# A matmul kernel for a hybrid decoder layer: weights asked for buffer by buffer, attention heads cut into more steps, gates' outcome in place

## The chip, the cores and the metric

The kernel runs on one core of a Trainium2 chip. The metric is the device time of one execution in microseconds (us); the kernel before takes 1519.82 us, the median of 3 runs (1517.38 to 1522.48). TensorE is PE in the profile, VectorE DVE, ScalarE ACT, GpSimd POOL, and SyncE, which issues most of the DMAs, SP.

## The reference, cut to what matters

```python
h = einsum('bsd,dc->bsc', x, w_in) + b_in             # 1024 tokens, 2048 -> 4352
q, k, v, g_attn, u_pool, g_pool = split(h)            # 16 heads of 64, 2 kv heads
a = banded_sink_attention(q, k, v, sinks, bias) * silu(g_attn)   # window 128
b = multiscale_pool(u_pool, w_pool, pool_scale) * silu(g_pool)
mix = einsum('bsc,cd->bsd', concat([a, b]), w_out)    # 2048 -> 2048
ple = sigmoid(x @ w_gate_ple) * (p @ w_ple)
return layer_norm(2**0.25 * x + mix + ple, ln_gain, ln_bias)
```

Everything is float32. In the attention, per head and block of 128 queries, the scores against the previous and the present 128 keys get a relative-position bias; the softmax takes a sink into its sum.

## The kernel before, in words

A float32 product is made of three matmuls in a reduced format: each operand is split into a high part (a cast on ACT) and a low part (a subtraction on DVE), and high x high, high x low and low x high are added in PSUM (`mm3`). Two blocks of 128 output rows and one half of the contraction make a *job*. Seven products (p1 to p7) of block sums take the place of eight, and a product is twelve matmuls with 512 columns. Their left operand is a *unit*: a 128x512 piece of the weights, or of sums of such pieces, split into `wh` (ACT, L213) and `wl` (DVE, L120) four products before its use (`take`, `units_to`). The raw weights come as two 512 KB buffers for a job out of a pool of five (`raw`). A job's results are gathered from the PSUM banks `qa`, `qb` and `sc` into an SBUF buffer `part` of 128x1024, by an ACT copy (L337) the first time and a DVE addition after that.

The stages, in order of time: two groups and then 25 jobs for the first projection (queries, keys and values first, then gates); 20 jobs for its other half of the contraction, where attention gates, pooling and the embedding are applied; the output projection in two halves; a last part with 256 columns; the layer norm. The program is written as one Python loop. A *tick* is the end of one product: `after(n, fn)` runs `fn` n ticks later, `later(n, fn)` does so too and puts its instructions behind the latest marked ones of PE, ACT and DVE. A scheduler then orders the instructions of each engine by when their inputs should be there, with the order of the program as priority; an engine runs its instructions strictly in that order.

Beside the first stage's last 24 jobs run the 16 attention heads, one every 9 ticks (`heads`). `begin` fetches a head's queries from DRAM (`s<-q`) and splits them at once, two casts on ACT (L479, L481) and two subtractions on DVE; `score` multiplies with the keys; `softmax` takes the exponential (ACT L516), adds the two halves (POOL), and scales by one over the sum (ACT L526); `trans` transposes. Small buffers `s` come from a pool of 16. In the same stretch `centre_weights` goes twice over half of w_out in 256 KB pieces through the only buffer `cw`: fetch, subtract the mean (DVE, L120), store to `wc`.

Where the second stage ends, the attention gates' last four blocks are done: `gate_ahead` fetches the attention results (`s<-pre`, two halves per block), `gate_attn` takes Silu of the part (ACT L586), multiplies the fetched halves in place (DVE, `s<-s,part`), and stores each half of 256 KB to `cc` with a DMA on POOL's queue. The pool of small buffers is cut to four there, and `gate_ahead` is called when a job's last product is done. At the first of the plain jobs `norm_scale` and then `norm_out` of the first layer norm are put between products.

Of the kernel before, what the change touches and what calls it, by code (L numbers as in the profile page):

```python
# [31 lines left out]
P = 128  # L32
T = 512
# [17 lines left out]
F1, F2 = 768, 256  # L51

# [10 lines left out]
class Layer:  # L63
    def __init__(self, ctx, tc, x, p, win, wgate, wout, wple, wpool, cst, rel, out):
        self.tc, self.nc = tc, tc.nc
        self.x, self.p, self.wple, self.wpool, self.rel, self.out = x, p, wple, wpool, rel, out
        self.win, self.wgate, self.wout = win, wgate, wout
        self.ctx = ctx
        self.dram = self.pool("dram", 1, space=DRAM)
        self.ps = self.pool("ps", 1, space=PSUM)  # L70
        self.fix = self.pool("fix", 1)
        self.sm = self.pool("sm", 3)
        self.wp = self.pool("w", 4)
        self.rp = self.pool("r", 5)
# [11 lines left out]
        self.n_raw = self.n_split = self.n_used = 0  # L86
# [101 lines left out]
    def load_raw(self, job):  # L188
        if id(job) not in self.raw:
            self.raw[id(job)] = [self.tile(self.rp, [P, 2 * H], "raw") for _ in range(2)]  # L190
            for i in range(2):
                self.load(self.raw[id(job)][i], job.w[job.b[i], job.half])

    def make_unit(self, i):
        job, o = self.seq[i]
        L, nc = self, self.nc
        self.load_raw(job)
        r0, r1 = self.raw[id(job)]
# [4 lines left out]
        if o in ("p5", "p6") and id(job) not in self.s1:  # L203

            s1 = self.s1[id(job)] = self.tile(self.sp, [P, H], "s1")
# [4 lines left out]
        src = {"p1": a11, "p2": a12, "p5": self.s1.get(id(job)), "p6": a11, "p7": a21, "p3": a12, "p4": a22,  # L210
# [5 lines left out]
        if o in ("p4", "a22"):  # L216
            self.raw[id(job)] = None
# [137 lines left out]
    def run_group(self, g, steps=(), then=None):  # L355

        jobs, order = self.groups[g]
        ahead = [j for js, _ in self.groups[g + 1 : g + 2] for j in js]
        st = {}
        for i, job in enumerate(jobs):  # L360
            self.load_raw(job)
# [48 lines left out]
    def run_plain(self, g):  # L410

        (job,), order = self.groups[g]
        self.load_raw(job)
        for js, _ in self.groups[g + 1 : g + 2]:
            self.load_raw(js[0])
        for i in range(2):
            ps = self.bank(BANKS[0][i], 2)[:, :F2]
            for u in range(2):
# [6 lines left out]
                self.mark("PE", mm)  # L425
                if u:
# [40 lines left out]
    def heads(self, h, j):  # L467
# [3 lines left out]
        qs, sc, pt, pv, pre, bias = [], {}, {}, {}, [], []  # L471

        def begin():
            rq = self.fetch(self.qd[j][:, h * T : h * T + T])
            bias.append(self.slot()[:, :T].rearrange("p (e k) -> p e k", e=2))
            self.load(bias[0], self.rel[j])
            qs.extend([self.slot(F32R), self.slot(F32R)])
            a, b = slice(0, 64), slice(64, 128)
            nc.scalar.copy(out=qs[0][a, :T], in_=rq[a, :T])  # L479
            self.lo(qs[0][b, :T], rq[a, :T], qs[0][a, :T])  # L480
            nc.scalar.copy(out=qs[1][b, :T], in_=rq[b, :T])  # L481
            self.lo(qs[1][a, :T], rq[b, :T], qs[1][b, :T])
# [29 lines left out]
        def softmax(bq):  # L512
# [57 lines left out]
        begin()  # L570
        for bq in range(4):
            t = 4 * (bq // 2)
            self.after(3 + 2 * bq, lambda bq=bq: score(bq))
            if bq % 2:
                self.after(7 + t, lambda bq=bq: shift(bq - 1))
                self.after(13 + t, lambda bq=bq: trans(bq - 1))
            self.after(8 + t, lambda bq=bq: softmax(bq))
            self.after(18 + t + bq % 2, lambda bq=bq: value(bq))
# [200 lines left out]
    def norm_scale(self, L):  # L779
# [16 lines left out]
        self.norm_spread(L, L["a"], self.ones, dg)  # L796
# [13 lines left out]
    def run(self):  # L810
# [63 lines left out]
        for j in s3:  # L874
            j.wait = 3 if j in s3[-2:] else 4
            j.ahead = self.embed_ahead if j.w is wgate else (lambda b: self.gate_ahead(b - GA0)) if j.b[0] < U0 else None
# [43 lines left out]
        for job in s1[:3]:  # L920
            self.raw[id(job)] = [self.tile(self.rp if job is not s1[2] or i else r1, [P, 2 * H], "raw") for i in range(2)]

        def piece(job, t, f):
            self.load(self.raw[id(job)][t][:, f], job.w[job.b[t], job.half][:, f])
# [53 lines left out]
        for i in range(16):  # L978
            self.after(t + 9 * i, lambda i=i: self.heads(i % 2, i // 2))
# [12 lines left out]
        for i in range(n3):  # L992
# [7 lines left out]
            if i == n3 - 1:  # L1000
# [190 lines left out]
```

## Time and profile before

| what | us |
|---|---|
| median of 3 runs | 1519.82 |
| profiled execution | 1519.77 |
| its span, first to last instruction | 1517.8 |
| TensorE busy | 1455.6 (96%) |
| VectorE busy | 1122.1 (74%) |
| ScalarE busy | 784.4 (52%) |
| GpSimd busy | 281.8 (19%) |
| mean granted TensorE clock | 0.985 |

The profiled execution is 0.05 us from the median, and 1.97 us of it lie outside the span. TensorE is the busiest engine by far, so what it waits for, and the stretches in which it runs at the lower clock, are what a change can take away without taking away matmuls. In a timeline the bracket at the end of a row gives the time that the engine sat idle before it, and who let it go.

### The profile page before, as it was taken

To read this page: it belongs to the slowest core of one execution; us is meant where nothing else is said; L and a number is where in the kernel's file an instruction comes from. 1 tells how busy PE (TensorE), PEld (TensorE's weight loads), DVE (VectorE), ACT (ScalarE), POOL (GpSimd) and SP (SyncE) were. 2 spreads that over 40 slices of the span, in tenths; PEclk is the share of its full clock that TensorE was granted. 3 is DMA by queue.
4 is the path that set the end of the run, shared out by engine and by line. 5 is a ranking of instruction groups with operands and counts; after the bars stand their busy time and mean duration, and the time that the engine had idled before them with its cause. 6 is when DMAs were issued, how large, how long until landed. Compare 5 with 4: busy or idle time off the path is not lost. (4 is left out here: it accounts for less than half of the span.)

```text
span 1517.8 us, 20491 instructions
## 1 busy us (share of the span) xinstructions
PE 1455.6 (96%) x6972; PEld 1227.7 (81%) x6972; DVE 1122.1 (74%) x2030; ACT 784.4 (52%) x1550; POOL 281.8 (19%) x396
## 2 busy tenths in 40 slices
PE   8999899999998999999999998999997999999986
PEld 6788688888877888878887786888886888899985
DVE  7787478788787788788666785565658766987786
ACT  5463556565655656566544453333336433554485
POOL 0001123323322333231111111000012111111240
PEclk9999999999999999999999999999999999999998
DMA  6563875445554456447767657675759578585564
GB/s 259 204 218 100 216 186 194 166 140 166 170 172 161 165 187 200 167 158 259 170 179 194 177 138 242 178 189 164 202 179 291 136 185 234 139 249 126 152 227 148
DMA packets 101848, 280.37 MB, mean 185 GB/s; under 512 B 11760, under 2 KB 17008, under 8 KB 101744
## 3 DMA queue, kind: packets, MB, share of 16 engines
q1 hardware_dynamic: 76400, 199.89, 39.4%
q0 software_dynamic: 19840, 67.64, 19.4%
q10 hardware_dynamic: 5504, 11.54, 2.2%
q8 instruction: 54, 0.88, 0.2%
q14 instruction: 50, 0.41, 0.1%
HBM read 193.04 MB, written 85.98 MB: 184 GB/s over the span
## 5 line engine op out<-in xcount | busy, mean ns | idle before, releaser
L213 ACT CAST wh<-raw 128x512 fp32r<-128x512 f32 x428 | 263.9, 619 | 404.1 <-PE qa L178 136.1
L120 DVE TENSOR_TENSOR wl<-raw,wh 128x512 fp32r<-128x512 f32 x428 | 296.4, 697 | 147.7 <-ACT wh L213 140.8
L337 ACT COPY part<-qa 128x512 f32<-128x512 f32 (+1 forms) x180 | 103.8, 577 | 42.9 <-PE qa L179 42.3
L542 POOL TENSOR_SCALAR_AFFINE_SELECT s<-s 128x512 fp32r<-128x512 f32 x128 | 102.1, 809 | 115.1 <-ACT s L535 84.2
L177 PE MATMUL qa<-t2h,wh 128*128 128x512 f32 (+1 forms) x260 | 102.5, 395 | 15.7 <-ACT wh L213 9.8
L120 DVE TENSOR_TENSOR part<-part,qb 128x512 f32<-128x512 f32 (+1 forms) x120 | 80.9, 674 | 47.7 <-PE qb L179 47.6
L177 PE MATMUL qa<-b11h,wh 128*128 128x512 f32 (+2 forms) x292 | 111.1, 381 | 2.1 <-ACT b11h L239 1.5
L179 PE MATMUL qa<-b11h,wl 128*128 128x512 f32 (+2 forms) x292 | 110.0, 377 | 1.1 <-DVE wl L120 1.1
L178 PE MATMUL qa<-b11l,wh 128*128 128x512 f32 (+2 forms) x292 | 110.0, 377 | 0.2 <-DVE b11l L120 0.2
L177 PE MATMUL qb<-b21h,wh 128*128 128x512 f32 (+2 forms) x292 | 109.1, 374 | 0.0
L179 PE MATMUL qb<-b21h,wl 128*128 128x512 f32 (+2 forms) x292 | 108.7, 372 | 0.1
L178 PE MATMUL qb<-b21l,wh 128*128 128x512 f32 (+2 forms) x292 | 108.6, 372 | 0.0
L179 PE MATMUL qa<-t2h,wl 128*128 128x512 f32 (+1 forms) x260 | 100.8, 388 | 4.0 <-DVE wl L120 4.0
L177 PE MATMUL qb<-t1h,wh 128*128 128x512 f32 (+1 forms) x260 | 101.8, 392 | 2.5 <-DVE part L120 1.1
L177 PE MATMUL qa<-t3h,wh 128*128 128x512 f32 (+1 forms) x260 | 101.0, 389 | 2.6 <-ACT part L337 2.5
L177 PE MATMUL qa<-t4h,wh 128*128 128x512 f32 (+1 forms) x260 | 100.5, 386 | 1.9 <-DVE part L120 1.9
L179 PE MATMUL qb<-t1h,wl 128*128 128x512 f32 (+1 forms) x260 | 100.5, 386 | 1.5 <-DVE wl L120 1.5
L177 PE MATMUL qb<-b22h,wh 128*128 128x512 f32 (+1 forms) x260 | 100.7, 387 | 0.0
L178 PE MATMUL qb<-t1l,wh 128*128 128x512 f32 (+1 forms) x260 | 100.4, 386 | 0.0
L178 PE MATMUL qa<-t2l,wh 128*128 128x512 f32 (+1 forms) x260 | 100.4, 387 | 0.0
L179 PE MATMUL qb<-b22h,wl 128*128 128x512 f32 (+1 forms) x260 | 99.8, 384 | 0.0
L178 PE MATMUL qa<-t4l,wh 128*128 128x512 f32 (+1 forms) x260 | 99.7, 384 | 0.0
(285 smaller groups left out, 3575.1 us busy)
## 6 DMA issues: line engine op xcount, KB each, us to landing
raw<-in_win SPq DMA_DIRECT2D x65, 512.0 KB, 4.1
h<-part SPq DMA_DIRECT2D x34, 512.0 KB, 3.0
part<-h POOLq DMA_DIRECT2D x34, 512.0 KB, 6.4
cw<-in_wout SPq DMA_DIRECT2D x64, 256.0 KB, 3.0
raw<-in_wgate SPq DMA_DIRECT2D x32, 512.0 KB, 4.1
raw<-wc SPq DMA_DIRECT2D x32, 512.0 KB, 4.4
s<-in_x SPq DMA_DIRECT2D x44, 256.0 KB, 5.0
wc<-cw SPq DMA_DIRECT2D x32, 256.0 KB, 2.2
```

Source lines behind the costliest of these rows:

```text
L120: return (eng or self.nc.vector).tensor_tensor(out=out, in0=a, in1=b, op=op)
L177: mm(ps, wh, xh, start=start, stop=False, skip_group_check=True)
L178: mm(ps, wh, xl, start=False, stop=False, skip_group_check=True)
L179: return mm(ps, wl, xh, start=False, stop=stop, skip_group_check=True)
L213: self.unit_latest = [nc.scalar.copy(out=hi, in_=src).ins, L.lo(lo, src, hi).ins]
L337: self.mark("ACT", self.nc.scalar.copy(out=dst, in_=ps))
L542: nc.gpsimd.affine_select(out=o4, in_=a4, pattern=[[0, 4], [sign, P]], compare_op=ALU.is_ge, fill=0.0, base=0 if side else -1, channel_mul ...
```

## The change

Raw weights: `load_raw`, which asks for both buffers of a job at a set product of the group before, becomes `feed_raw`, which after every product asks for the next buffer if the unit that last reads the buffer five before has been made (`freed`, `ring`).

Heads: `begin` comes a tick earlier and only fetches; the casts and subtractions of the queries become `split`, three ticks later and behind the marked instructions. The scaling by one over the sum becomes `share`, two ticks after `softmax` and behind the marked instructions. The rest of a head stays at the same tick as before.

Gates: the product goes into the part (`c[:, h]`), and one 512 KB DMA stores both halves. For the last two jobs `gate_ahead` is called 4 to 7 ticks after the last group begins, not when a job ends; the small pool there has 6 buffers of 512 columns in place of 4 of 528, and `two` 8 in place of 9.

Layer norm: the spreading matmuls of the first `norm_scale` come two ticks later, and `norm_out` runs from tick 7 on, two a tick, in place of 3 in two ticks from tick 5.

```diff
-    def load_raw(self, job):
-        if id(job) not in self.raw:
-            self.raw[id(job)] = [self.tile(self.rp, [P, 2 * H], "raw") for _ in range(2)]
-            for i in range(2):
-                self.load(self.raw[id(job)][i], job.w[job.b[i], job.half])
+    def feed_raw(self, until=None):
+        while self.to_feed:
+            job, i = self.to_feed[0]
+            if self.ring[-RAWS] not in self.freed and (until is None or (until, 1) in self.ring):
+                return
+            self.to_feed.pop(0)
+            t = self.tile(self.rp, [P, 2 * H], "raw")
+            self.raw.setdefault(job, []).append(t)
+            self.load(t, job.w[job.b[i], job.half])
+            self.ring.append((job, i))
...
-        if o in ("p4", "a22"):
-            self.raw[id(job)] = None
+        if o in ("p3", "a12", "p4", "a22"):
+            self.freed.add((job, int(o in ("p4", "a22"))))
...
                 self.product(job, o, st[job])
-                if i == (0 if g else 2) and job is jobs[-1]:
-                    for j in ahead:
-                        self.load_raw(j)
+                self.feed_raw()
...
         def begin():
-            rq = self.fetch(self.qd[j][:, h * T : h * T + T])
+            rq.append(self.fetch(self.qd[j][:, h * T : h * T + T]))
             bias.append(self.slot()[:, :T].rearrange("p (e k) -> p e k", e=2))
             self.load(bias[0], self.rel[j])
+
+        def split():
+            q = rq[0]
             qs.extend([self.slot(F32R), self.slot(F32R)])
-            nc.scalar.copy(out=qs[0][a, :T], in_=rq[a, :T])
+            nc.scalar.copy(out=qs[0][a, :T], in_=q[a, :T])
...
             if z == 0:
                 self.tt(cur, old, cur, ALU.add, nc.gpsimd)
+
+        def share(bq):
+            cur = sc[bq][:, :, P:]
             for e in range(2):
...
         begin()
+        self.later(3, split)
...
-            self.after(3 + 2 * bq, lambda bq=bq: score(bq))
+            self.after(4 + 2 * bq, lambda bq=bq: score(bq))
...
-            self.after(8 + t, lambda bq=bq: softmax(bq))
-            self.after(18 + t + bq % 2, lambda bq=bq: value(bq))
+            self.after(9 + t, lambda bq=bq: softmax(bq))
+            self.later(11 + t, lambda bq=bq: share(bq))
+            self.after(19 + t + bq % 2, lambda bq=bq: value(bq))
...
         for h, pre in enumerate(self.got.pop(("ga", j))):
-            f = slice(h * T, h * T + T)
-            self.tt(pre, pre, c[:, h], ALU.mult)
-            self.aside(self.cc[j // 2][:, j % 2, f], pre)
+            self.tt(c[:, h], pre, c[:, h], ALU.mult)
+        self.aside(self.cc[j // 2][:, j % 2], c.rearrange("p h t -> p (h t)"))
...
+        spread = lambda: self.norm_spread(L, L["a"], self.ones, dg)
+        if wait:
+            self.later(wait, spread)
...
-            self.after(t + 9 * i, lambda i=i: self.heads(i % 2, i // 2))
+            self.after(t - 1 + 9 * i, lambda i=i: self.heads(i % 2, i // 2))
...
-                self.slots = self.work_pool("slots1", 4, work)
-                self.twos = self.work_pool("twos1", 9, work)
+                self.slot_n = T
+                self.slots = self.work_pool("slots1", 6, work)
+                self.twos = self.work_pool("twos1", 8, work)
                 pooled()
+                for n, b in enumerate(b for j in s3[-2:] for b in j.b):
+                    self.after(4 + n, lambda b=b: self.gate_ahead(b - GA0))
...
-        self.later(4, lambda: self.norm_scale(one))
+        self.later(4, lambda: self.norm_scale(one, 2))
         for j in range(NB):
-            self.later(5 + (2 * j) // 3, lambda j=j: self.norm_out(one, j))
+            self.later(7 + j // 2, lambda j=j: self.norm_out(one, j))
```

How the change moves instructions is seen at three places. The names carry a buffer's number, the brackets name what an instruction waits for (DMAHW and DMASW are DMAs of SP and of POOL, PE, DVE, Activation and Pool the engines), and "..." stands for rows left out.

First place: ACT in the second group of the second stage, where the first head begins. Before, the queries' casts (`s_1620`, `s_1621`) stand among the units and ahead of the keys' build (`kh`) and of the copies `part<-qa`:

```order
L213 CAST wh_1510<-raw_1426 128x512 [waits DVE_49,PE_49]
L479 CAST s_1620<-s_1616 64x512 [waits DMAHW7_49]
L213 CAST wh_1536<-raw_1426 128x512 [waits DVE_49,PE_49,Activation_49]
L481 CAST s_1621<-s_1616 64x512
L213 CAST wh_1571<-s_359_1531 128x512 [waits PE_49,Activation_49]
L337 COPY part_1407<-qa_1412 128x512 [waits PE_49]
L123 ACTIVATE s_1506<-s_1506,cst 64x512 [waits DMASW6_49]
L123 ACTIVATE s_1507<-s_1507,cst 64x512 [waits DMASW7_49,DMASW5_49,DMASW3_49]
L442 CAST kh_362_1556<-s_1506 64x512 [waits Activation_49]
L442 CAST kh_362_1556<-s_1506 64x512
...
L337 COPY part_1569<-qa_1575 128x512 [waits DMASW2_49,DMASW0_49,PE_49]
```

In the changed kernel:

```order
L222 CAST wh_1516<-raw_1312 128x512 [waits DVE_49,PE_49]
L222 CAST wh_1542<-raw_1312 128x512 [waits DVE_49,PE_49,Activation_49]
L222 CAST wh_1577<-s_362_1537 128x512 [waits PE_49,Activation_49]
L346 COPY part_1413<-qa_1418 128x512 [waits PE_49]
L125 ACTIVATE s_1512<-s_1512,cst 64x512 [waits DMASW6_49]
L125 ACTIVATE s_1513<-s_1513,cst 64x512 [waits DMASW7_49,DMASW5_49,DMASW3_49]
...
L445 CAST kh_367_1569<-s_1513 64x512
L346 COPY part_1575<-qa_1581 128x512 [waits DMASW2_49,DMASW0_49,PE_49]
...
L346 COPY part_1576<-qb_1660 128x512 [waits DMAHW5_49,PE_49]
L485 CAST s_1676<-s_1596 64x512 [waits DMAHW7_49]
L487 CAST s_1677<-s_1596 64x512
```

The two casts (now L485 and L487) have gone behind the keys' build and behind the copies of both banks, some twenty rows later.

Second place: SP in the middle of the heads, in the second pass of `centre_weights` over w_out. Before:

```order
L134 DMA cw_4527<-in_wout 128x512 [waits DMAHW1_49,DMAHW0_49]
L134 DMA raw_4789<-in_wgate 128x1024 [waits DVE_49]
L134 DMA wc_207<-cw_4527 128x512 [waits DMAHW3_49,DMAHW1_49,DVE_49]
L134 DMA raw_5034<-in_wgate 128x1024 [waits DMAHW4_49,DVE_49]
L134 DMA cw_4599<-in_wout 128x512 [waits DMAHW3_49]
L134 DMA pre_157<-s_4496 128x512 [waits DMAHW6_49,DVE_49]
L134 DMA wc_208<-cw_4599 128x512 [waits DMAHW7_49,DMAHW5_49,DVE_49]
```

In the changed kernel:

```order
L136 DMA g_131<-part_4252 128x1024 [waits Activation_49]
L136 DMA cw_4523<-in_wout 128x512 [waits DMAHW7_49,DMAHW1_49]
L136 DMA wc_207<-cw_4523 128x512 [waits DMAHW2_49,DMAHW1_49,DVE_49]
L136 DMA raw_4591<-in_wgate 128x1024 [waits DMAHW3_49,DVE_49]
L136 DMA cw_4599<-in_wout 128x512 [waits DMAHW2_49]
L136 DMA raw_4639<-in_wgate 128x1024 [waits DVE_49]
```

The store `wc_207<-cw` stood between two raw loads, with the next `cw` fetch behind the second of them; now store, raw load, fetch, raw load follow each other.

Third place: where the second stage ends. ACT before, with the four Silus (L586) of the gates' last parts and the first copies into the next group's parts:

```order
L337 COPY part_10796<-qa_10818 128x512 [waits PE_49]
L586 ACTIVATE part_10484<-part_10484,cst 128x1024 [waits DMASW0_49]
L586 ACTIVATE part_10485<-part_10485,cst 128x1024 [waits DMASW2_49,Activation_49]
L213 CAST wh_10847<-s_2128_10842 128x512 [waits DVE_49]
L337 COPY part_10798<-qa_10851 128x512 [waits DVE_49,PE_49,Activation_49]
L586 ACTIVATE part_10486<-part_10486,cst 128x1024 [waits DMASW1_49]
L586 ACTIVATE part_10487<-part_10487,cst 128x1024 [waits DMASW3_49]
L239 CAST t2h_10928<-two_10506 128x1024 [waits DVE_49]
L239 CAST t2h_10928<-two_10507 128x1024 [waits DVE_49]
```

In the changed kernel:

```order
L346 COPY part_10794<-qa_10816 128x512 [waits DMASW3_49,PE_49]
L597 ACTIVATE part_10484<-part_10484,cst 128x1024 [waits DMASW4_49]
L597 ACTIVATE part_10485<-part_10485,cst 128x1024 [waits DMASW6_49,Activation_49]
L248 CAST t2h_10918<-two_10506 128x1024 [waits DVE_49]
L346 COPY part_10796<-qa_10847 128x512 [waits DMASW0_49,PE_49,Activation_49]
L597 ACTIVATE part_10486<-part_10486,cst 128x1024 [waits DMASW5_49]
L597 ACTIVATE part_10487<-part_10487,cst 128x1024 [waits DMASW7_49]
L222 CAST wh_10882<-s_2135_10877 128x512 [waits DVE_49]
L222 CAST wh_10900<-raw_10375 128x512 [waits PE_49]
L248 CAST t2h_10918<-two_10507 128x1024
L346 COPY part_10795<-qb_10930 128x512 [waits DMASW1_49,PE_49,Activation_49]
```

The copies `part<-qa` and `part<-qb` now wait for DMAs of POOL (the stores of the gates' outcome out of the part that they are to fill), and one of them stands ahead of the last two Silus. SP at the same place, before:

```order
L134 DMA raw_10534<-in_wout 128x1024 [waits DMAHW4_49,DVE_49]
L134 DMA raw_10537<-in_wout 128x1024 [waits DMAHW5_49,DVE_49]
L134 DMA raw_10538<-in_wout 128x1024 [waits DMAHW6_49,DVE_49]
L134 DMA raw_10865<-in_wout 128x1024 [waits DMAHW7_49,DVE_49]
L134 DMA s_10787<-pre_160 128x512 [waits DMAHW0_49,DMASW4_49,DVE_49]
L134 DMA s_10789<-pre_160 128x512 [waits DMAHW1_49,DMASW5_49,DVE_49]
L134 DMA s_10792<-pre_161 128x512 [waits DMAHW2_49,DMASW6_49,DVE_49]
L134 DMA s_10794<-pre_161 128x512 [waits DMAHW3_49,DMASW7_49,DVE_49]
```

In the changed kernel:

```order
L136 DMA s_10634<-pre_160 128x512 [waits DMAHW7_49]
L136 DMA s_10636<-pre_160 128x512 [waits DMAHW0_49]
L136 DMA raw_10680<-in_wout 128x1024 [waits DMAHW6_49,DVE_49]
L136 DMA raw_10716<-in_wout 128x1024 [waits DMAHW7_49,DVE_49]
L136 DMA raw_10718<-in_wout 128x1024 [waits DMAHW0_49,DVE_49]
L136 DMA raw_10737<-in_wout 128x1024 [waits DMAHW1_49,DVE_49]
L136 DMA s_10659<-pre_161 128x512 [waits DMAHW2_49,DVE_49]
L136 DMA s_10661<-pre_161 128x512 [waits DMAHW3_49,DVE_49]
```

The fetches of the attention's results (`s<-pre`) wait for no DMA of POOL any more, and six of the eight are ahead of the four raw loads, where four were.

## Rows read from the trace of the kernel before

**Rows 1.** The page, part 1: busy time, share of the span, instructions.

```profile
PE 1455.6 (96%) x6972; PEld 1227.7 (81%) x6972; DVE 1122.1 (74%) x2030; ACT 784.4 (52%) x1550; POOL 281.8 (19%) x396
```

**Rows 2.** Windows, by stretch: length, then each engine's busy time, granted clock, DMA share.

```profile
170.00:185.00 15.00, 9.52 (x35) 7.35 (x35) 8.13 (x13) 10.01 (x18) 0.89 (x1) 0.77 0.63 135
405.00:435.00 30.00, 27.68 (x138) 22.78 (x137) 23.05 (x56) 20.49 (x51) 9.84 (x14) 1.00 0.54 185
475.00:485.00 10.00, 4.91 (x20) 4.48 (x21) 7.04 (x16) 5.05 (x12) 2.85 (x4) 0.66 0.56 195
630.00:640.00 10.00, 8.41 (x43) 6.85 (x42) 5.22 (x12) 4.07 (x7) 1.96 (x4) 1.00 0.64 221
665.00:685.00 20.00, 17.53 (x84) 14.12 (x83) 13.25 (x31) 12.68 (x35) 8.90 (x11) 1.00 0.49 154
1165.00:1185.00 20.00, 12.13 (x42) 9.11 (x41) 18.49 (x25) 8.46 (x12) 2.70 (x5) 0.74 0.40 135
```

**Rows 3.** Waits of ACT and DVE: total us, times, longest.

```profile
ACT s L479 <- DMA s<-q: 39.8, 13, 8.7
DVE cw L120 <- DMA cw<-in_wout: 12.1, 7, 4.7
```

**Rows 4.** Timeline of ACT, 162 to 179 us: start, length, instruction, idle before.

```profile
172.08 0.62 ACT L479 CAST s<-s 64x512 fp32r<-64x512 f32 x1 [8.69 <-DMA s<-q]
174.89 1.33 ACT L123 ACTIVATE s<-s,cst 64x512 f32<-64x512 f32 x2
176.12 2.53 ACT L442 CAST kh<-s 64x512 fp32r<-64x512 f32 x4
178.68 0.59 ACT L337 COPY part<-qa 128x512 f32<-128x512 f32 x1
```

**Rows 5.** Timeline of PE at the same place.

```profile
173.44 0.39 PE L179 MATMUL qb<-b21h,wl 128*128 128x512 f32 x1
179.32 0.79 PE L177 MATMUL qa<-t2h,wh 128*128 128x512 f32 x1 [5.49 <-ACT part L337]
184.33 0.60 PE L454 MATMUL tr<-ident,s 128*128 128x128 f32 x4
```

**Rows 6.** Timeline of SP at the same place: the store and the fetch.

```profile
159.51 2.10 SPq L134 DMA_DIRECT2D q<-part  x2
167.05 0.32 SPq L134 DMA_DIRECT2D s<-q  x1
```

**Rows 7.** Timeline of PE, 420 to 426 us.

```profile
424.88 0.33 PE L500 MATMUL sc<-kl,s 128*128 128x128 f32 x1 [1.04 <-DVE kl L120]
```

**Rows 8.** Timeline of SP, 463 to 470 us: the centring's store and next fetch.

```profile
463.60 0.33 SPq L134 DMA_DIRECT2D wc<-cw  x1
469.55 0.33 SPq L134 DMA_DIRECT2D cw<-in_wout  x1
```

**Rows 9.** Timeline of DVE, 472 to 478 us.

```profile
472.73 0.69 DVE L120 TENSOR_TENSOR cw<-cw,wmean 128x512 f32<-128x512 f32 x1 [4.67 <-DMA cw<-in_wout]
```

**Rows 10.** Timeline of PE, 474 to 485 us.

```profile
480.09 1.11 PE L454 MATMUL tr<-ident,s 128*128 128x128 f32 x4 [5.16 <-DVE s L120]
```

**Rows 11.** Timeline of SP, POOL, DVE and PE where the stage of gates ends.

```profile
1165.48 3.88 SPq L134 DMA_DIRECT2D s<-pre  x4
...
1162.53 1.23 POOL L139 DMA_DIRECT2D cc<-s  x2 [3.30 <-DVE s L120]
...
1170.57 1.41 DVE L120 TENSOR_TENSOR s<-s,part 128x512 f32<-128x512 f32 x2 [0.58 <-DMA s<-pre]
...
1175.74 0.80 PE L177 MATMUL qa<-t2h,wh 128*128 128x512 f32 x1 [1.15 <-ACT wh L213]
```

**Rows 12.** DMA issues: KB each and median us to landing.

```profile
cc<-s POOLq DMA_DIRECT2D x32, 256.0 KB, 4.1
co<-part POOLq DMA_DIRECT2D x16, 512.0 KB, 5.8
```

**Rows 13.** Timeline of PE at the first layer norm's scale.

```profile
1455.32 1.56 PE L776 MATMUL sc<-q,ones 128*128 128x512 f32 x4 [1.34 <-ACT q L794]
```

More of the change, by code (lines that the diff above doesn't have):

```diff
@@ L51 @@
 F1, F2 = 768, 256
+RAWS = 5
 class Job:
@@ L196, in make_unit @@
         L, nc = self, self.nc
-        self.load_raw(job)
-        r0, r1 = self.raw[id(job)]
+        if len(self.raw.get(job, ())) < 2:
+            self.feed_raw(job)
+        r0, r1 = self.raw[job]
         a11, a12, a21, a22 = r0[:, :H], r0[:, H:], r1[:, :H], r1[:, H:]
@@ L202, in make_unit @@
             behind.enter_context(self.tc.issue_after(ins))
-        if o in ("p5", "p6") and id(job) not in self.s1:
-            s1 = self.s1[id(job)] = self.tile(self.sp, [P, H], "s1")
+        if o in ("p5", "p6") and job not in self.s1:
+            s1 = self.s1[job] = self.tile(self.sp, [P, H], "s1")
             L.tt(s1, a21, a22, ALU.add)
@@ L209, in make_unit @@
             L.tt(a12, a12, a11, ALU.subtract)
-        src = {"p1": a11, "p2": a12, "p5": self.s1.get(id(job)), "p6": a11, "p7": a21, "p3": a12, "p4": a22,
+        src = {"p1": a11, "p2": a12, "p5": self.s1.get(job), "p6": a11, "p7": a21, "p3": a12, "p4": a22,
                "a11": a11, "a12": a12, "a21": a21, "a22": a22}[o]
@@ L357, in run_group @@
         jobs, order = self.groups[g]
-        ahead = [j for js, _ in self.groups[g + 1 : g + 2] for j in js]
         st = {}
         for i, job in enumerate(jobs):
-            self.load_raw(job)
             st[job] = dict(tags=BANKS[i], out=[self.new_part(b) for b in job.b], filled=job.filled)
@@ L425, in run_plain @@
                 self.mark("PE", mm)
+                self.feed_raw()
                 if u:
@@ L470, in heads @@
         mx, neg, sk, den, rec = (st[:, 8 * i : 8 * i + 8] for i in range(5))
-        qs, sc, pt, pv, pre, bias = [], {}, {}, {}, [], []
+        rq, qs, sc, pt, pv, pre, bias = [], [], {}, {}, {}, [], []
         def begin():
-            rq = self.fetch(self.qd[j][:, h * T : h * T + T])
+            rq.append(self.fetch(self.qd[j][:, h * T : h * T + T]))
             bias.append(self.slot()[:, :T].rearrange("p (e k) -> p e k", e=2))
             self.load(bias[0], self.rel[j])
+        def split():
+            q = rq[0]
             qs.extend([self.slot(F32R), self.slot(F32R)])
             a, b = slice(0, 64), slice(64, 128)
-            nc.scalar.copy(out=qs[0][a, :T], in_=rq[a, :T])
-            self.lo(qs[0][b, :T], rq[a, :T], qs[0][a, :T])
-            nc.scalar.copy(out=qs[1][b, :T], in_=rq[b, :T])
-            self.lo(qs[1][a, :T], rq[b, :T], qs[1][b, :T])
+            nc.scalar.copy(out=qs[0][a, :T], in_=q[a, :T])
+            self.lo(qs[0][b, :T], q[a, :T], qs[0][a, :T])
+            nc.scalar.copy(out=qs[1][b, :T], in_=q[b, :T])
+            self.lo(qs[1][a, :T], q[b, :T], qs[1][b, :T])
         def k0(bq):
@@ L777, in norm_spread, with norm_scale @@
             self.nc.scalar.activation(out[:, i:e], ps, AF.Copy, scale=scale)
-    def norm_scale(self, L):
+    def norm_scale(self, L, wait=0):
         nc, n = self.nc, L["n"] // P
@@ L875, in run @@
             j.wait = 3 if j in s3[-2:] else 4
-            j.ahead = self.embed_ahead if j.w is wgate else (lambda b: self.gate_ahead(b - GA0)) if j.b[0] < U0 else None
+            j.ahead = self.embed_ahead if j.w is wgate else (lambda b: self.gate_ahead(b - GA0)) if j.b[0] < U0 and j.wait == 4 else None
         mixed = [(wout, *p) for p in pairs(0, 8)]
@@ L920, in run @@
         for job in s1[:3]:
-            self.raw[id(job)] = [self.tile(self.rp if job is not s1[2] or i else r1, [P, 2 * H], "raw") for i in range(2)]
+            self.raw[job] = [self.tile(self.rp if job is not s1[2] or i else r1, [P, 2 * H], "raw") for i in range(2)]
+        every = [(j, i) for js, _ in self.groups for j in js for i in range(2)]
+        self.ring = [k for k in every[:6] if k != (s1[2], 0)]
+        self.to_feed = every[6:]
         def piece(job, t, f):
-            self.load(self.raw[id(job)][t][:, f], job.w[job.b[t], job.half][:, f])
+            self.load(self.raw[job][t][:, f], job.w[job.b[t], job.half][:, f])
         lo, up, all_ = slice(0, H), slice(H, 2 * H), slice(0, 2 * H)
```

15 lines of the change are left out of this document (7 added, 8 removed).

## The prediction

> **What bounds the kernel now.** I read the busy times first: TensorE works 96% of the span [rows 1], so only the other 4%, some 60 us, and the stretches at the lower clock can be won; the change takes no matmul away. Then I laid windows over the span and kept those in which PE falls short of its window and in which the changed code runs [rows 2]. The reader is to see two kinds: windows at clock 1.00 that miss 1 to 3 us, and three (170–185, 475–485, 1165–1185) that miss 5 to 8 us and have a clock of 0.66 to 0.77 besides. The waits then say who stands in the way: ACT's cast of a head's queries waits 39.8 us for the fetch, DVE's centring 12.1 us for its piece of w_out [rows 3]. Both engines run in order, so what counts is what is queued behind. The timelines at the three places give that.
>
> **The change, part by part.** The sum is made against the profiled execution, 1519.77 us, which is 0.05 us from the median of the runs.
>
> *Queries' split, first head.* Two queries' stores start at 159.51 and the fetch that reads one back can only go at 167.05 [rows 6]. ACT stands 8.69 us for it, until 172.08 [rows 4]. Behind the cast are queued three units, two bias additions (1.33 us), four casts of keys (2.53) and the copy that empties a `qa` bank (178.68); PE waits 5.49 us for that copy and starts at 179.32 [rows 4, 5]. In the new order both query casts are behind the copies. What ends last then: the units need inputs that were there by about 167 (the cast at 172.08 is the only thing that kept them), the keys' bias additions can begin when the keys have landed, which I put at 169.4 (sent as the stores before it end, at 163.8, and an estimate of 5 to 6 us under way), then 1.33 + 2.53 + 0.59 plus a unit or two in between: the copy ends near 173.9 and PE loses 0.4 us of the 5.5. Gain 5.1. The twelve matmuls after the stall took 179.32 to 184.33, 5.0 us, where a product takes 2.7 at the full rate (twelve starts of 0.227 us apart, as at 173.44 and before); 2.3 us go to the lower of the two clock levels. Without the stall that goes too, mostly: I take 1.9. Term: −7.0, between −7.5 and 0 (if the keys land late, the copy is where it was).
>
> *Queries' split, the other heads.* Fifteen more fetches share the remaining 31 us of ACT's waits [rows 3], nearly all hidden by the units made four products ahead. Where they reached PE: 1.04 us at 424.88 [rows 7], where the low keys of the second build were late behind such a wait, and 1.59 in 630–640 (10.00 − 8.41) [rows 2], where ACT sat behind a query cast too. Term: −2.6, between −2.6 and 0. A fetch begins a tick earlier, but it waits for a small buffer that PE and POOL of an older head give back, so the fetch gains less than the tick; the three ticks between fetch and cast are what counts.
>
> *Share.* The same number of ACT scalings, two ticks later, with more than ten ACT instructions still between them and the transposition's cast. 665–685 misses 2.47 us [rows 2], where scalings that waited for POOL held up a copy. It could give up to −1.9, and could cost as much where a scaling now stands ahead of a unit. Term: 0.
>
> *Raw weights by buffer.* Every load was already issued by SP when its buffer came free, in the same order; the new code puts most of them at the same place among PE's instructions, the rest within two products. Nothing to win on SP, nothing added: 0, between −1 and +1. What it does move is the neighbourhood on SP's queue, the next term.
>
> *The centring's stall.* SP sends the store `wc<-cw` at 463.60, a raw load after it, and can send the next fetch into the only `cw` only when the store has landed, at 469.55 [rows 8]. DVE stands 4.67 us on the subtraction until 472.73 [rows 9]; behind it are queued the sums of the next unit, so its `wh`, so PE: 5.16 us, until 480.09 [rows 10], and 475–485 has a clock of 0.66 [rows 2], which I price at 2 us as at the first head. At stake: 7. In the new order the store is sent ahead of that raw load, and the fetch ahead of the next. But the pattern "raw, store, raw" occurs five times in SP's order of either kernel, and only one of the five reached PE before. Term: −5, between −7 and 0.
>
> *New stalls in the heads' stretch.* All instructions of 15 heads are shuffled against the loads. The four windows between 405 and 685 miss 2.3, 5.1, 1.6 and 2.5 us [rows 2], mean 2.9: I put one of that kind back. Term: +3, between 0 and +8.
>
> *Gates in place, loads ahead.* Before, the last four `s<-pre` go out from 1165.48 on, when the small buffers' stores (`cc<-s`, 1162.53) have landed; DVE stands at their products until 1170.57 with sums of raw weights queued behind, and PE starts at 1175.74 [rows 11]; the window misses 7.9 us, and the clock is 0.74 [rows 2]. The last product before ends near 1167.1 (1175.74 less the window's 7.9 and a lone matmul), so the loss is 8.6 + 2.3 = 10.9, the second term as at the first head. In the new order the fetches don't wait for the stores, so DVE has no such wait. But the result now lies in the part, and the next group's copies into these parts wait for the 512 KB store: ACT has such a copy ahead of the last two Silus and of two units. Stores of 256 KB land in 4.1 us, of 512 KB from a part in 5.8 [rows 12]. Sent near 1162.8, the first lands at 1168.6, the copy, two Silus (2.2) and the DVE work behind them follow; PE resumes with one product at about 1168.8 and waits again up to 4 us. I get 7 to 8 us lost in place of 10.9. Term: −3, between −7 (no wait) and +6 (a store that takes twice the 5.8 us of the row, for each of two copies, and the lower clock again).
>
> The Trainium skill, DMA: Bandwidth & Descriptors, section Anatomy of one DMA, gives a fixed cost of about 2.0 us for each transfer and the rest by bandwidth; by it two halves joined into one would save a fixed cost, and 512 KB would land in some 3.2 us (an estimate from that page), the gates' term would be about −5.6. The rows have 5.8 us for that size, so I go by them.
>
> *Layer norm.* PE waits 1.34 us for the scale's diagonal at 1455.32 [rows 13]; two ticks later it is there, but `norm_out` is then pressed into fewer ticks, on ACT and DVE that are both busy there. Term: −0.7, between −1.5 and +1.5.
>
> Sum: −7.0 − 2.6 − 5 + 3 − 3 − 0.7 = −15.3, so 1519.77 − 15.3 = 1504.5 us. The start, the end and the DMA-bound wait about 905–925 are not touched.
>
> **Rivals.**
> *The stall moves.* The centring's wait stays or falls on another of the five patterns, and the shuffle adds two stalls: −7.0 − 2.6 + 0 + 6 − 3 − 0.7 = −7.3, 1512.5. For it: nothing in the change frees the one `cw` buffer earlier than its store lands. Against: four of five such patterns were hidden.
>
> *The change doesn't do what it says.* The loads are in the old order, the first head's copy waits for the keys, the gates' store eats what the fetches gave: only the 2.6 and 0.7 are left, 1516.5, within 0.3% (4.6 us), which I take as what can't be told from no change. For it: the keys come over POOL's queue in a stretch where the DMA engines are busy 0.63 of the time [rows 2]; against: the row of 8.69 names the query and not the keys.
>
> *Slower: small buffers.* A head's fetch and its bias now take two of the 16 small buffers a tick earlier, while value and the last reads stay, so each head holds them 2.7 us longer. SP is in order: if the fetch then stands for the older head's POOL and PE work, the raw loads behind it come late, and a unit with them. It decides once SP stands longer than the raw loads are ahead; beyond it, one stall the size of the 630–640 one (1.6) at each of 15 heads is 24 us: 1519.8 − 15.3 + 24 = 1528.5. Against: the raw weights have five buffers, two for a job of seven products, and none of the windows of before [rows 2] has PE waiting for a raw load.
>
> **How the numbers follow.** Forecast 0.62 (its own range 1497 to 1510), the stall moves 0.20, no effect 0.12, slower 0.06. Range 1496 to 1517: the lower end is the sum with the centring at −7 and no new stall; the upper takes in the second and third case. Faster by over 0.3% needs less than 1515.2: 0.62 + 0.20 = 0.82; within 0.3% 0.12; slower by over 0.3% 0.06.
>
> **What would show it.** First head: in 170–185 PE busy over 14 us and the clock at 1.00, no wait of ACT for `s<-q` of several us anywhere. Centring: DVE's longest wait for `cw` under 3 us. Gates: PE's idle time about 1165–1185 falls to 6 us or less, and the largest wait there is ACT's copy into a part for a store of POOL's queue, not DVE's for `s<-pre`. Layer norm: no wait of PE for the diagonal. Wrong would be: several waits of 2 us and more on PE between 200 and 700 that before doesn't have, or SP standing at `s<-q` with raw loads late behind.

## The result, and the profile after

The changed kernel takes 1504.80 us (median of 4 runs, 1503.65 to 1509.39), the kernel before 1518.60 beside it (4 runs, 1516.68 to 1522.48): ratio 0.9912, 95% interval 0.9882 to 0.9941, so 0.9% faster and clear of the noise. The profiled execution has a span of 1502.8 us, 15.0 less than before, and TensorE is as busy as it was, in a shorter span. The page, part 1:

```profile
PE 1453.8 (97%) x6972; PEld 1225.5 (82%) x6972; DVE 1119.7 (75%) x2030; ACT 781.1 (52%) x1550; POOL 278.9 (19%) x388
```

To find where the time went, look up the start of the same product in both timelines and subtract. Each line below is one product; the last column is what the stretch since the line above won or lost.

| start before | start after | after − before | stretch | won (−) or lost (+) |
|---|---|---|---|---|
| 48.55 | 48.22 | −0.33 | start | −0.3 |
| 184.68 | 176.59 | −8.09 | first head | −7.8 |
| 469.66 | 463.17 | −6.49 | heads up to the centring's stall | +1.6 |
| 487.84 | 474.64 | −13.20 | the centring's stall | −6.7 |
| 704.14 | 689.60 | −14.54 | the other heads | −1.3 |
| 1100.96 | 1088.80 | −12.16 | second stage | +2.4 |
| 1156.04 | 1146.80 | −9.24 | just before the gates end | +2.9 |
| 1183.82 | 1169.24 | −14.58 | end of the gates | −5.3 |
| 1439.07 | 1424.03 | −15.04 | output projection | −0.5 |

Every stretch is read from one profile of each kernel. After the last line nothing changes: the span's end is 15.0 earlier too. Windows of the changed kernel, laid over the same times as five of [rows 2] (columns as there; each lies some us further on in the program):

```profile
170.00:185.00 15.00, 15.00 (x72) 12.09 (x71) 10.86 (x21) 12.07 (x21) 0.35 (x1) 1.00 0.89 243
405.00:435.00 30.00, 29.03 (x145) 24.07 (x144) 24.75 (x60) 21.26 (x52) 9.57 (x11) 1.00 0.51 181
475.00:485.00 10.00, 9.73 (x50) 8.06 (x49) 7.30 (x17) 6.93 (x17) 0.77 (x2) 1.00 0.53 172
630.00:640.00 10.00, 9.52 (x54) 8.11 (x53) 9.79 (x19) 4.32 (x10) 0.75 (x1) 1.00 0.72 244
665.00:685.00 20.00, 20.00 (x97) 16.68 (x96) 14.19 (x23) 8.52 (x17) 6.34 (x8) 1.00 0.86 282
```

The first is full, the third nearly, where 5 us and the clock were missing, and the clock is 1.00 in all. ACT's timeline at the first head, which answers to [rows 4]:

```profile
168.45 0.58 ACT L346 COPY part<-qa 128x512 f32<-128x512 f32 x1
168.93 1.34 ACT L125 ACTIVATE s<-s,cst 64x512 f32<-64x512 f32 x2
170.16 2.54 ACT L445 CAST kh<-s 64x512 fp32r<-64x512 f32 x4
172.73 0.59 ACT L346 COPY part<-qa 128x512 f32<-128x512 f32 x1
...
180.55 0.63 ACT L485 CAST s<-s 64x512 fp32r<-64x512 f32 x1
```

The query's fetch still goes out at 166.78, as in [rows 6]; its cast simply stands at 180.55, behind the copy, and no row of waits has ACT standing for `s<-q` any more (39.8 us in [rows 3]). At the centring's stall DVE waits 0.26 us for the piece, not 4.67 [rows 9], and PE 0.41 us, not 5.16 [rows 10]:

```profile
461.12 0.69 DVE L122 TENSOR_TENSOR cw<-cw,wmean 128x512 f32<-128x512 f32 x1 [0.26 <-DMA cw<-in_wout]
...
470.64 0.66 PE L457 MATMUL tr<-ident,s 128*128 128x128 f32 x4 [0.41 <-DVE s L122]
```

Elsewhere DVE still waits for `cw`, 3.93 us at 672.37 and 2.68 at 408.85, and no matmul stands behind these two waits.

What is new is a small wait at the scores. The list of waits, and the largest of them on PE:

```profile
PE sc L506 <- DVE s L122: 5.2, 11, 1.2
...
448.60 0.33 PE L506 MATMUL sc<-kh,s 128*128 128x128 f32 x1 [1.21 <-DVE s L122]
```

Split and score are one tick apart now, and where ACT is late PE waits for the low half of the queries. The brackets show only a part of the price. From the start of the matmul before to the start of a `sc<-kh` matmul it is 29.1 us in all for the 144 of them, where it was 21.1: 8.0 us more, about half of it up to the centring's stall and half after it. That the heads' two rows of the table come to +1.6 and −1.3 all the same is due to older waits that are gone, the three largest of them after the centring:

```profile
639.70 0.50 PE L177 MATMUL qa<-t4h,wh 128*128 128x512 f32 x1 [1.59 <-DVE part L120]
670.67 0.50 PE L177 MATMUL qa<-t3h,wh 128*128 128x512 f32 x1 [0.61 <-ACT part L337]
675.54 0.50 PE L177 MATMUL qa<-t3h,wh 128*128 128x512 f32 x1 [1.85 <-ACT part L337]
```

Where the gates end, POOL, ACT and PE of the changed kernel:

```profile
1154.01 0.56 POOL L141 DMA_DIRECT2D cc<-part  x1 [4.78 <-DVE part L122]
...
1157.73 0.59 ACT L346 COPY part<-qa 128x512 f32<-128x512 f32 x1 [0.31 <-DMA cc<-part]
...
1158.82 0.47 PE L179 MATMUL qb<-t1h,wh 128*128 128x512 f32 x1 [0.98 <-DVE part L122]
1163.44 0.50 PE L179 MATMUL qa<-t2h,wh 128*128 128x512 f32 x1 [1.38 <-ACT wh L222]
```

PE waits 3.4 us here (a third wait of 1.02 at 1164.96), where it waited 7.9 before; the granted clock is 0.92 in the window of the changed kernel, 0.74 in that of [rows 2]:

```profile
1150.00:1172.00 22.00, 18.61 (x73) 14.36 (x72) 21.39 (x30) 12.90 (x18) 2.19 (x4) 0.92 0.45 147
```

The copy does wait for the store of its part, but 0.31 us only: the store lands within 3.7 us. The price is paid some 30 us earlier, on ACT:

```profile
1116.19 4.28 ACTq L267 DMA_DIRECT2D two<-cc  x4
1120.56 0.59 ACT L346 COPY part<-qb 128x512 f32<-128x512 f32 x1 [3.75 <-DMA s<-pre]
1123.51 4.63 ACTq L267 DMA_DIRECT2D two<-cc  x2
1128.18 0.62 ACT L222 CAST wh<-raw 128x512 fp32r<-128x512 f32 x1 [7.04 <-DMA two<-cc]
```

and so on PE:

```profile
1130.35 0.50 PE L179 MATMUL qa<-t3h,wh 128*128 128x512 f32 x1 [3.09 <-ACT part L346]
```

ACT issues the eight fetches of the pooled operand itself. Five `s<-pre` fetches are now sent by SP at the same moment (from 1116.35 on, a sixth at 1123.79), where four were; and ACT stands at its issues until earlier DMAs have landed, with units and copies queued behind. The semaphores in the trace tell which. The DMAs of SP and of ACT signal the same eight semaphores in turn (a wait for DMAHW in an order view can be for a DMA of either), and an issue waits for the earlier DMA on its semaphore. ACT's issue at 1123.51 waits for an `s<-pre` of SP that was sent at 1116.72 and has landed at 1123.45, the one at 1127.62 for ACT's own `two<-cc` of 1116.90, landed at 1127.60. ACT stood at this place before the change too, but only once, and no matmul waited for it:

```profile
1137.94 0.59 ACT L337 COPY part<-qb 128x512 f32<-128x512 f32 x1 [5.68 <-DMA s<-pre]
```

### The profile page after: what moved, and what is told of

Its sections match the earlier page's. It is cut to its first block, busy times and chain, and to the rows that moved or that the text cites. A ratio compares the mean times of both kernels' runs of the same rounds, so it can differ in the third digit from the quotient of the medians.

```text
span 1502.8 us, 20461 instructions
## 1 busy us (share of the span) xinstructions
PE 1453.8 (97%) x6972; PEld 1225.5 (82%) x6972; DVE 1119.7 (75%) x2030; ACT 781.1 (52%) x1550; POOL 278.9 (19%) x388
## 5 line engine op out<-in xcount | busy, mean ns | idle before, releaser
L181 PE MATMUL qa<-t4h,wl 128*128 128x512 f32 (+1 forms) x260 | 99.7, 383 | 0.0
L180 PE MATMUL qa<-t3l,wh 128*128 128x512 f32 (+1 forms) x260 | 99.7, 383 | 0.0
```

The source lines that it names most:

```text
L180: mm(ps, wh, xl, start=False, stop=False, skip_group_check=True)
L181: return mm(ps, wl, xh, start=False, stop=stop, skip_group_check=True)
```

## The experiments

Theory A: the change wins three separate stalls (first head, centring, end of the gates) and adds two (scores, ACT's issues); the raw loads are issued where they were. Rivals: the gain comes from the raw loads; it comes from reordering as such; the part held by the store is what limits the gates. First each part of the change alone, on the kernel before.

**Raw weights by buffer alone** (the changed kernel with `heads`, the gates and the layer norm as before). 

> The raw weights by buffer alone, all else as before. Theory A (each stall has its own cause, and the loads are issued in the old order anyway): within 2 us of before, ACT's wait of about 8.7 us for the first head's query, DVE's wait for cw of 4 to 5 us and the stall of about 8 us at the end of the gates all still there. Rival B (what is won comes from the raw loads lying elsewhere on SP's queue): the cw stall is gone, 5 to 8 us faster than before.

1522.80 us (1515.73 to 1528.70, 10 runs) against 1519.29, ratio 1.0023, interval 1.0002 to 1.0043: no gain, and 3.5 us of loss by the medians (0.3 to 6.5 by the interval), more than the 2 us that theory A allows. ACT's and DVE's waits stay:

```profile
ACT s L482 <- DMA s<-q: 36.1, 12, 11.5
DVE cw L122 <- DMA cw<-in_wout: 9.4, 6, 4.4
```

The products stand in the same order and start up to 6.5 us later, 2.9 of it from the first head on, where ACT stands 11.49 us for the query and PE 8.27. PE's stall of 7.9 us at the end of the gates is there too. Rival B falls.

**Queries' split alone.**

```diff
+        self.later(3, split)
...
-            self.after(3 + 2 * bq, lambda bq=bq: score(bq))
+            self.after(4 + 2 * bq, lambda bq=bq: score(bq))
...
-            self.after(t + 9 * i, lambda i=i: self.heads(i % 2, i // 2))
+            self.after(t - 1 + 9 * i, lambda i=i: self.heads(i % 2, i // 2))
```

The later steps of a head move by a tick with `score`, as in the change.

> Before, with only the heads' queries fetched a tick earlier and split three ticks later (share, gates, raw loads, norm as before). Theory A: the first head's stall of 5.5 us and its low clock go, as do the 1.0 and 1.6 us at other query casts, and the scores wait for the low queries instead, at most 1 us each and 4 to 6 us in all; the time is 6 to 10 us less than before, more if the cw stall goes with it. Rival B (reordering as such, not the split): the stall of the first head goes, but two or more new stalls of 2 us come, and the time is within 4 us of before.

1508.47 us, ratio 0.9923 (0.9902 to 0.9943), 10.8 us less. As theory A has it, the first head's stall is gone and the waits at the scores are there (4.9 us, 13 of them), and the centring's stall went with it:

```profile
474.21 0.66 PE L454 MATMUL tr<-ident,s 128*128 128x128 f32 x4 [0.46 <-DVE s L120]
```

**Share alone.**

```diff
-            for e in range(2):            # at the end of softmax(bq)
+        def share(bq):
+            for e in range(2):
...
+            self.later(10 + t, lambda bq=bq: share(bq))
```

> Before, with only the scaling by one over the sum put two ticks behind softmax. Theory A: 0 to 2 us less than before; the first head's stall stays at 5 to 6 us of PE. Rival B (the share unblocks ACT, and is what takes the cw stall away): DVE's longest wait for cw under 3 us and 5 to 8 us less than before.

1510.08 us, ratio 0.9932 (0.9914 to 0.9950), 9.2 us less. Each theory is right in a half: the first head's stall stays, as theory A has it, and the centring's stall falls to 1.48, as rival B has it. DVE's longest wait for `cw` is still 4.1 us, but it is another one, at 679.31, and no matmul stands behind it:

```profile
182.08 0.79 PE L177 MATMUL qa<-t2h,wh 128*128 128x512 f32 x1 [7.65 <-ACT part L337]
...
477.71 0.66 PE L454 MATMUL tr<-ident,s 128*128 128x128 f32 x4 [1.48 <-DVE s L120]
```

PE's two waits of 0.61 and 1.85 us at 670 to 676 are one of 0.27 here. So share is worth more than the 0 that the prediction gave it, and split and share each take the centring's stall, which can be won once.

**Gates in place and fetches ahead alone** (that part of the diff above, all of it). 

> Before, with only the gates' outcome in place, one store a block, and the fetches ahead with six small buffers. Theory A: the stall of 8 us at the end of the gates shrinks to 2 to 4 us, and a wait of 2 to 4 us of ACT's copy into a part for a store comes about 25 us earlier: 2 to 5 us less than before. Rival B (the part held by the store costs as much as the fetches win): within 1 us of before.

1517.67 us, ratio 0.9988 (0.9976 to 0.9999): 1.6 us by the medians, between rival B's 1 and theory A's 2. The stall at the end of the gates is 3.65 us in three waits, and PE loses 1.92 us at 1140.55 for ACT's copy, which stands behind ACT's DMA issues and not, as theory A had it, for a store.

**The centring a tick earlier**, on the kernel before.

```diff
-        self.centre_weights(8, 3)
+        self.centre_weights(7, 3)
```

> Before, with the centring of w_out begun a tick earlier and nothing else. Theory A (the cw stall is a coincidence of this store with a raw load on SP's queue, and any shift takes it away): the stall of 4 to 5 us at 480 falls below 2 us, the first head's stall stays, 5 to 8 us less than before. Rival B (the one cw buffer is the cause and stalls wherever it is put): PE stalls 3 us or more at another centring, within 2 us of before.

1520.14 us, ratio 1.0007 (0.9990 to 1.0024). The stall shrinks, but stays at its place:

```profile
465.67 0.69 DVE L120 TENSOR_TENSOR cw<-cw,wmean 128x512 f32<-128x512 f32 x1 [2.68 <-DMA cw<-in_wout]
...
478.73 0.66 PE L454 MATMUL tr<-ident,s 128*128 128x128 f32 x4 [3.57 <-DVE s L120]
```

Neither theory is right as it was put. A shift by itself doesn't take it away. Beside each other, the waits of DVE for `cw` in that group and of PE behind it are 4.67 and 5.16 (before), 2.68 and 3.57 (here), 0.53 and 1.48 (share alone), 0.26 and 0.41 (the change): PE's wait follows DVE's and is up to 1 us longer. What differs is how early DVE gets to the subtraction before it, which in the two main kernels is

```profile
462.89 0.68 DVE L120 TENSOR_TENSOR cw<-cw,wmean 128x512 f32<-128x512 f32 x1
...
450.78 0.68 DVE L122 TENSOR_TENSOR cw<-cw,wmean 128x512 f32<-128x512 f32 x1
```

From one subtraction to the next the piece must be stored, the store must land, the next piece must be fetched and land, all through the one buffer. That takes 9.84 us before (462.89 to 472.73), 8.26 here, 7.54 with share alone and 10.34 in the changed kernel (450.78 to 461.12): the change doesn't shorten it. For 5.2, 5.6, 7.0 and 10.1 us of it, in this order, DVE is at other instructions or waits for their inputs; it waits for the piece in what is left.

**In place only**, and **ahead only**, on the kernel before, one run each.

```diff
+            self.tt(c[:, h], pre, c[:, h], ALU.mult)                    # in place only
+        self.aside(self.cc[j // 2][:, j % 2], c.rearrange("p h t -> p (h t)"))
...
+                self.slots = self.work_pool("slots1", 6, work)           # ahead only
...
+                    self.after(4 + n, lambda b=b: self.gate_ahead(b - GA0))
```

> Before, with the gates' outcome in the part and one store a block, four small buffers and the late fetches kept. Theory A (in place alone frees the small buffers at once, since DVE's product and no store releases them, so the fetches at the job's end still come 3 to 4 us too late): the stall at the end of the gates is 3 to 6 us, between the 7.9 of before and the 3.4 of the change. Rival B (only fetching ahead matters): 7 us or more.

> Before, with the fetches ahead and six small buffers, the product kept in the fetched buffers and two stores a block. Theory A (the last two fetches still wait for the stores): the stall at the end of the gates is 4 to 7 us. Rival B (six buffers and early fetches are enough): under 3.4 us, as in the change or less.

In place only: 1516.26 us; PE's waits there are 1.04, 1.42, 1.45 and 0.73, 4.6 us in all, not far from the 3.4 of the change. Ahead only: 1517.90 us; 5.69 us there, and 2.90 us at 1140.46. The times of single runs decide nothing (the kernel before has 1516.39 to 1523.63 beside them); both stalls are as theory A has them.

```profile
1168.56 0.47 PE L177 MATMUL qb<-t1h,wh 128*128 128x512 f32 x1 [1.04 <-DVE part L120]
1172.95 0.50 PE L177 MATMUL qa<-t2h,wh 128*128 128x512 f32 x1 [1.42 <-ACT wh L213]
1174.90 0.80 PE L177 MATMUL qa<-t2h,wh 128*128 128x512 f32 x1 [1.45 <-ACT wh L213]
1176.43 0.79 PE L177 MATMUL qb<-t1h,wh 128*128 128x512 f32 x1 [0.73 <-DVE part L120]
```

The product in place does most of the work at the end of the gates. The early fetches take 1 to 2 us more off there and bring the stall at 1130, which in place only doesn't have. By the starts of the same products between 1101 and 1200 us, in place only wins 3.1 us, both together 3.0, and ahead only loses 1.0: in these profiles the early fetches are worth nothing.

Then the changed kernel, with one thing altered at a time.

**Split at two ticks** (`self.later(2, split)`). 

> The changed kernel with the queries' split two ticks after the fetch in place of three. Theory A (the scores wait for the low queries because split and score are only a tick apart): the sum of PE's waits at the scores for the low queries, 5.2 us, falls below 1.5 us, no wait of ACT over 3 us for the fetch comes back, and the time is 3 to 5 us less than that of the changed kernel. Rival B (the three ticks are what keeps the first head free): ACT stands for the first head's query again, over 3 us, PE stalls about 173 us, and the time is 2 to 5 us more.

1502.43 us, ratio to before 0.9886 (0.9849 to 0.9922). Theory A's mechanism holds: PE has no wait at the scores for the low queries left in the list, and the first head stays free, the cast standing at 179.42. By the time alone it can't be told from the changed kernel; in the profile the product that starts at 803.53 in the changed kernel starts 7.9 us earlier, at 795.6, and 4.3 of these are lost again by the end of the gates: 1.2 where PE waits for the embedding's input (6.45 us, 5.28 in the changed kernel), the rest mostly to the lower clock, granted 0.89 in 1120 to 1135 and 0.77 in 1155 to 1170 us, where the changed kernel has 1.00 and 0.89 at about the same products (1126 to 1142 and 1160 to 1175).

**Operand fetches by SP.**

```diff
-                    (nc.sync if first else nc.scalar).dma_start(out=t, in_=src)
+                    nc.sync.dma_start(out=t, in_=src)
```

> The changed kernel with the fetches two<-cc issued by SP, not by ACT. Theory A (the new stall of 3.1 us at 1130 comes from ACT standing at these issues while the s<-pre fetches, now ahead, take the DMA engines): ACT has no wait of 7 us for two<-cc and the stall at 1130 is gone, 2 to 4 us less than the changed kernel. Rival B (it comes from the part buffers held by the 512 KB stores): the stall stays at 2 us or more, within 1 us of the changed kernel.

The edit also moves eight of the earlier `two<-in_x` fetches to SP. 1501.82 us, ratio 0.9886 (0.9846 to 0.9927), by the time alone not to be told from the changed kernel. The stall of 3.09 us at 1130 is gone, with 1.05 us at 1142.98 in its place, which shows that theory A has its cause right: ACT's issues, and not the parts held by the stores. A wait of 2.97 us comes at 1203.16, where DVE stands 6.23 us for a fetch `part<-r` (0.52 in the changed kernel):

```profile
1195.70 1.23 DVE L122 TENSOR_TENSOR csum<-csum,part 128x1024 f32<-128x1024 f32 x1 [6.23 <-DMA part<-r]
...
1203.16 0.50 PE L179 MATMUL qa<-t4h,wh 128*128 128x512 f32 x1 [2.97 <-DVE part L122]
```

**Layer norm as before** (spread at once, `norm_out` from tick 5). 

> The changed kernel with the layer norm's spread and outcome at the ticks of before. Theory A: PE waits about 1.3 us for the diagonal again, in place of 0.4, the small waits of the last stage are 3 us in all as in the changed kernel (which has 3.5): within 1.5 us of the changed kernel. Rival B (denser norm_out is what costs): 1 to 3 us less than the changed kernel.

1503.70 us, ratio 0.9893 (0.9859 to 0.9926): not to be told from the changed kernel. This edit does nothing that shows.

**Without share.** 

> The changed kernel with the scaling by one over the sum back in softmax. Theory A (split and share each do away with the cw stall, since each moves DVE's and SP's order there, and it is won once only): the cw stall doesn't come back, the time is within 3 us of the changed kernel and close to the run with the split alone less the gates' gain. Rival B (the gains add up): 6 to 9 us more than the changed kernel.

1510.14 us (1506.44 to 1517.00, 10 runs), ratio 0.9938 (0.9917 to 0.9958), 5 us above the changed kernel by the medians and between the two expectations; the intervals of the two ratios overlap. The centring's stall doesn't come back (0.45 us), so rival B falls there. In the profiles 2.9 us are lost up to 665, in the heads, where waits of 0.65 and 0.57 us for ACT's copy are back; 1 us more by 913, at the embedding's input (7.39 us); and 3.3 more by 1133, where the stall at ACT's issues is 4.77 us and the lower clock follows it (0.89 granted in 1130 to 1146). So share is worth about 3 us by itself in the heads, by this pair of profiles; that the later losses come from it is not shown.

**Three of them together**: split at two ticks, fetches by SP, layer norm as before. 

> The changed kernel with the queries' split at two ticks, the fetches two<-cc by SP, and the layer norm's ticks of before. Theory A (the three stalls are apart): 1498 to 1500 us, 4 to 7 us less than the changed kernel. Rival B (a stall that goes comes back at the next of the engines): within 2 us of the changed kernel.

1497.34 us (1495.45 to 1501.22), ratio to before 0.9859 (0.9834 to 0.9884), some 7 us below the changed kernel, by medians of different comparisons, a little more than theory A has; the intervals of the two ratios just touch. The waits at the scores are gone:

```profile
PE sc L506 <- DVE s L122: 0.2, 1, 0.2
```

What is left in it are 2.98 us at 1201.90, as with the fetches by SP alone, and 1.92 us at the centring. It beats the kernel before clearly; that it beats the changed one is likely, but stands at the edge of the intervals.

## Why the prediction was right, point by point

The time was 1504.8 us where 1504.5 were predicted. By difference it is 13.8 us of the medians and 15.0 of the profiles, where 15.3 were forecast. The largest term, the first head, came by the mechanism told; that the sum hits so closely is luck, since several terms miss and make up for each other. The terms, beside the table above:

- First head, −7.0: −7.8, and by the mechanism told: the cast behind the copy, the stall and the lower clock gone. The copy that was to end at 173.9 ends at 173.3. The stall of the kernel without the split varies, 5.0 to 8.3 us in the profiles of the runs that keep it, as the query's fetch lands earlier or later.
- Other queries' casts −2.6, share 0, new stalls +3, together +0.4: +1.6 and −1.3, together +0.3. The sum is right by compensation. Of the other queries' casts the two waits of 1.04 and 1.59 us are gone, as told. So are the 0.61 and 1.85 at 670 to 676, for which share was given 0 though up to −1.9 was weighed; share gives some 3 us. The new stalls cost 8.0 us and not 3. They are not accidental ones, as the prediction had them, but waits at the scores with one cause that it could have seen: split and score are a tick apart. With the split at two ticks the 8.0 us are gone (20.8 us for the same matmuls).
- The centring, −5 of 7: −6.7. That the stall would go was right, the reason was not. SP sends store, raw load and fetch in this order in both kernels (463.60, 464.20 and 469.55 before; 451.49, 452.15 and 454.99 in the changed kernel), and the run with the centring a tick earlier sends them so too and keeps 3.57 us. The way through the one buffer is no shorter than before; DVE has 10.1 us of other work in it in place of 5.2. The sign that was named, DVE's longest wait for `cw` under 3 us, did not come: 3.93 us at 672.37, without a matmul behind it.
- Raw weights by buffer, 0, between −1 and +1: no gain, as told. Alone they cost 3.5 us (0.3 to 6.5); in that run's profile 2.9 us of it are the first head's stall, which the split removes. What they cost inside the change is not shown.
- Gates, −3: −5.3 and +2.9, together −2.4. The size is right, the reason is wrong. The largest wait was to be a copy into a part for the 512 KB store, landing in 5.8 us; the store landed within 3.7 us and the copy waited 0.31. What took the gain back is ACT, held at its own DMA issues by fetches that had not landed, those sent ahead among them. A smaller stall at this place, 1.22 and 1.34 us, is in the runs with the split alone and share alone too, where nothing is sent ahead, so the place is tight without them. The lower clock follows this stall in other runs (0.89 granted in 1120 to 1135 us with the split at two ticks) and not in the changed kernel's profile (1.00 in 1126 to 1142), so its price is at the low end there, by luck. The prediction counted DVE and the store and left out what the six earlier fetches do to the DMAs that ACT issues at that time. The estimate made there from the Trainium skill, DMA: Bandwidth & Descriptors, section Anatomy of one DMA (some 3.2 us for 512 KB), is nearer to this store, 3.7 us or less, than the median of another store that was used in its place. The same store at 1116 to 1118 us took 5.9 and 9.2 us.
- Layer norm, −0.7: nothing. PE's wait for the diagonal falls from 1.34 to 0.43 us, but the products before and after the stage are both 15.0 us earlier than before, so it is given back there; PE's waits for units behind the denser `norm_out` are some 0.4 us more.
- The second stage, 0: +2.4, in two waits that the prediction didn't look at, 1.37 us at 802.04 and 0.63 at 849.66, both of matmuls of the embedding that wait for DVE.

Of the rivals, "the stall moves" came true in small, at the scores and at ACT's issues; "small buffers" did not show, no raw load stood late behind a query's fetch.

## What to carry to other kernels

On an engine that runs in order, put an instruction that waits for a DMA behind those that don't need it. Then look who consumes its result: with three ticks the consumer stood one tick behind and waited, with two it did not, and the first head stayed free all the same. A fetch sent early is not free: it lands beside the DMAs of the same moment, and if a compute engine issues those, that engine can stand still until earlier ones have landed. A buffer that takes 8 to 10 us from use to use costs nothing as long as its engine has that much other work between the uses. Two edits that each remove the same stall don't add; alone they gave 11 and 9 us, with the rest of the change 14 to 15.

## What the runs showed of the hardware

A compute engine that issues DMAs can be held for long at an issue that waits for earlier DMAs to land: ACT stood 7.04 us at two issues of 512 KB in a stretch in which the DMA engines moved 259 GB/s on the mean (1105 to 1150 us), which no busy time shows. Stores of the same size land in very different times in one kernel: 3.7 us or less for `cc<-part` at 1154 us, 7.6 us (median of two) for the same store at 1116 to 1118.
